# Output projection and last product with tokens on the partitions, and 8 of the last product's 22 K-tile pairs by seven block products for eight

## The chip, the cores and the metric

The kernel runs on one core of one Trainium2 chip. The core has a matrix engine (PE, whose loading of the stationary operand the profile lists apart as PEld), a vector engine (DVE), a scalar engine (ACT), a general engine (POOL) and an engine that issues DMAs (SP). They run side by side and wait for each other by semaphores. The metric is the device time of one execution in microseconds (us), smaller being better.

## The reference

One decoder layer for 256 tokens (S) of 2048 features (D), all float32. Only the last two of its products matter here:

```python
x = x + jnp.einsum('bsd,de->bse', merged, w_out[l])          # output projection, 2048 x 2048
h2 = rmsnorm(x, norm2_g[l])
u = causal_dwconv(jnp.einsum('bsd,df->bsf', h2, w_up[l]), conv_w[l], conv_b[l])
u_gate, u_val = u[..., :D_FF], u[..., D_FF:]                 # D_FF = 5632
x = x + jnp.einsum('bsf,fd->bsd', jax.nn.silu(u_gate) * u_val, w_down[l])   # last product, 5632 x 2048
```

Ahead of them stand a norm, the input projection, an attention, an mLSTM, gates and two projections, which the change leaves as they are.

## The kernel before

Every large product is made exact to float32 by three passes: each operand is split into a high part (its rounding to float32r) and a low part (the exact rest), and high times high, high times low and low times high are summed in PSUM. The activations' parts are made once. The weights' parts are made as the weights come: `load_chunk` fetches 1 MB (128 partitions x 2048 columns) into `raw`, of which there are three; `split_sub` makes two pieces of 1024 columns of it, ACT writing the high part `wh` (L104) and DVE the rest `wl` (L105), each of which also has three buffers; `next_sub` gives PE the next piece and has later ones loaded and split.

There are two forms of product. In the form of `block_a` the weights stand still in PE and the activations move: for a K-tile (128 rows of the sum) and 128 output columns, one matmul over 512 moving columns (high and low part of the 256 tokens side by side) and one over 256 (`wl` with the high part), in `products_a`; the result has output columns on the partitions, in two halves that are added. The branch gates (g), the branch projections (p), the output projection (wo), the first feed-forward product (up) and, written out by hand, the last product (y) have this form. In the form of `block_b` the activations stand still, 128 tokens at a time, and the weights move: for a K-tile, 128 tokens and 512 output columns, three matmuls over 512 columns each (`product_b`); the result has tokens on the partitions. The attention's fq, fk, fv and the mLSTM's mv have this form.

Stages of the end of the kernel. wo (L605 to L615): 16 blocks of 128 columns; DVE adds each to the residual `x2` (features on the partitions) and ACT and DVE make from it the operand `h2` of the next product, while POOL sums squares (`add_square`). up (L642 to L653): 88 blocks; DVE and ACT evacuate each (`up_evac`: sum of the halves, scale, three taps of the convolution), and from each pair of blocks one K-tile of the last product comes, in `g_tiles`. Two matmuls and a small product in PE make the norm's factor per token on every partition (`norm`, `as_rows`), between the first blocks. y (L656 to L675): four blocks of 512 output columns over 44 K-tiles; after each, DVE adds the result to `x2` and SP stores it.

Each engine works its instructions off in the order in which the program's scheduler left them, which is not quite the order of the code: it moves instructions ahead of others on which they don't depend. So a wait at the head of an engine's list holds what stands behind it.

Of the kernel before, what the change touches and what calls it, by code (L numbers as in the profile page):

```python
# [17 lines left out]
P = 128  # L18
# [23 lines left out]
def trunk(ctx: ExitStack, tc: tile.TileContext, a):  # L42
# [5 lines left out]
    work = ctx.enter_context(tc.tile_pool(name="work", bufs=2))  # L48
    psacc = ctx.enter_context(tc.tile_pool(name="psacc", bufs=4, space=bass.MemoryType.PSUM))
# [17 lines left out]
    # ---------------------------------------------------------------- weights, in order of use  # L67
    chunks = []

    def add_b(ap, n):  # L70
        for i in range(ap.shape[0]):
            chunks.append((ap[i], 4 * n))

    for i in range(8):
        chunks.append((a["w_mog0"][i], 2 * (MOG[0] + MOG[1])))
    add_b(a["w_mog1"], MOG[2])
    for name in ("w_fox", "w_mqk", "w_mv", "w_g", "w_p", "w_out", "w_up", "w_dn"):
        add_b(a[name], 512)

# [3 lines left out]
    def load_chunk(i, part=None):  # L83
        """Chunk i, whole or as its halves one by one."""
        if i >= n_chunk or (i in raws and part != 1):
            return
        src, n = chunks[i]
        if i not in raws:
            raws[i] = wpool.tile([P, 2048], F32, tag="raw", bufs=3, name=f"raw{i}")
        c = slice(0, n) if part is None else slice(part * n // 2, (part + 1) * n // 2)  # L90
        nc.sync.dma_start(raws[i][:, c], src[:, c])

    def split_sub(j):
        i, s = divmod(j, 2)
        if i >= n_chunk or j in subs:
            return
        load_chunk(i)
        if j < KD:
            put(hT[:, j, 0, :], hT[:, j, 1, :], xT[:, j, :], cst[:, C_G1 + j : C_G1 + j + 1])
        n = chunks[i][1] // 2  # L100
        raw = raws[i][:, s * n : (s + 1) * n]
        wh = wpool.tile([P, 1024], F32R, tag="wh", bufs=3, name=f"wh{j}")
        wl = wpool.tile([P, 1024], F32R, tag="wl", bufs=3, name=f"wl{j}")
        nc.scalar.activation(wh[:, :n], raw, AF.Copy)  # L104
        nc.vector.tensor_tensor(wl[:, :n], raw, wh[:, :n].bitcast(F32), ALU.subtract)  # L105
        subs[j] = (wh[:, :n], wl[:, :n])
# [3 lines left out]
    def next_sub():  # L110
        j = state["sub"]
        state["sub"] = j + 1
        for c in range(j // 2, j // 2 + 3):
            load_chunk(c)
        for q in range(j, j + 2):
# [20 lines left out]

    def mm(out, lhsT, rhs, start, stop):
        nc.tensor.matmul(out, lhsT, rhs, start=start, stop=stop)  # L138

    def product_b(outs, act, k, wh, wl, first, last):  # L140
        """outs[tok] += act[k].T @ w for both blocks of tokens; outs and w as lists over columns."""
        for tok in range(2):
            t = slice(tok * P, (tok + 1) * P)
            for o, w in zip(outs[tok], wh):
                mm(o, act[:, k, 1, t], w, first, False)
            for o, w in zip(outs[tok], wh):
                mm(o, act[:, k, 0, t], w, False, False)
            for o, w in zip(outs[tok], wl):
                mm(o, act[:, k, 0, t], w, False, last)
# [16 lines left out]
    def products_a(z, act, ks, wh, wl, first, last):  # L166
        """z += w.T @ act over the K-tiles ks: [columns, tokens], the low part's product apart."""
        for q, k in enumerate(ks):
            ws = slice(q * P, (q + 1) * P)
            mm(z, wh[:, ws], act[:, k].rearrange("p l s -> p (l s)"), first and q == 0, False)  # L170
            mm(z[:, :S], wl[:, ws], act[:, k, 0, :], False, last and q == len(ks) - 1)
# [16 lines left out]
    # ---------------------------------------------------------------- loads and constants  # L188
# [4 lines left out]
    hT = big.tile([P, KD, 2, S], F32R, tag="actT", bufs=2, name="hT")  # L193
# [5 lines left out]
    # The tensor engine's clock rises while it works: it works on zeros until the data is there.  # L199
# [27 lines left out]
    # A row of float32 values over tokens is added to a product by one bfloat16 pass: its three  # L227
    # bfloat16 parts are exact, head h's lying on partitions h, 32 + h and 64 + h.
# [11 lines left out]
    def bf16_parts(parts, rest):  # L240
        """Three bfloat16 parts that sum to rest exactly; rest is overwritten."""
# [5 lines left out]
    def rsqrt_mean(out, ss, n, tmp):  # L247
        """out = (ss / n + eps) ** -0.5"""
# [3 lines left out]
    # ---------------------------------------------------------------- norms over the features  # L252
# [4 lines left out]
    def add_square(x, first):  # L257
        """sq += x * x, the squares of a K-tile, to be summed over the partitions."""
# [7 lines left out]
    def norm(r):  # L266
        """r[token] = 1 / rms of the token's features."""
# [6 lines left out]
    def as_rows(r):  # L274
        """rb = the per-token values r on every partition."""
# [7 lines left out]
    # ---------------------------------------------------------------- input projection  # L283
# [3 lines left out]
    def gate_evac(z, n, at, c0):  # L287
        """The output gates of n columns, the first c0 of them being the heads' gates."""
# [23 lines left out]
    # Gates: log forget gates, their running sums F, and the mLSTM's running maximum.  # L312
# [6 lines left out]
    def gates_a():  # L319
# [8 lines left out]
        # log1p(e) = log(u) + (e - (u - 1)) / u  # L328
# [47 lines left out]
    att = big.tile([P, 8192], F32, tag="actT", bufs=2, name="att")  # L376
    qT = att[:, 0:2048].rearrange("p (h s) -> p h s", h=FH)
    kT = att[:, 2048:4096].rearrange("p (h s) -> p h s", h=FH)
    fv = att[:, 4096:6144].rearrange("p (t e) -> p t e", t=2)
    mqT = att[:, 6144:7168].rearrange("p (h s) -> p h s", h=MH)  # L380
    mkT = att[:, 7168:8192].rearrange("p (h s) -> p h s", h=MH)
# [46 lines left out]
    # ---------------------------------------------------------------- forgetting attention  # L428
# [53 lines left out]
    # ---------------------------------------------------------------- mLSTM inputs  # L482
# [91 lines left out]
    # ---------------------------------------------------------------- branch gates  # L574
# [9 lines left out]
    # ---------------------------------------------------------------- branch projections  # L584
    am = big.tile([P, 16, 2, S], F32R, tag="actT", bufs=2, name="am")
    for k in range(0, 16, 2):
        put(am[:, k : k + 2, 0, :], am[:, k : k + 2, 1, :], amT[:, k : k + 2, :])
# [4 lines left out]
    mT = big.tile([P, KD, 2, S], F32R, tag="actT", bufs=2, name="mT")  # L592
    for j in range(KD):
# [9 lines left out]
        put(mT[:, j, 0, :], mT[:, j, 1, :], ms[0])  # L603

    # ---------------------------------------------------------------- output projection  # L605
    x2 = big.tile([P, KD, S], F32, tag="r16", bufs=3, name="x2")
    for q in range(4):
        nc.gpsimd.dma_start(x2[:, 4 * q : 4 * q + 4, :], a["xT"][:, 4 * q : 4 * q + 4, :])
    h2 = big.tile([P, KD, 2, S], F32R, tag="actT", bufs=2, name="h2")
# [8 lines left out]
    g_tiles = []  # L618
    for n, tag, bufs in ((16, "actT", 2), (8, "r16", 3), (8, "r16", 3), (4, "og", 1), (4, "mv", 1)):
        t = big.tile([P, n, 2, S], F32R, tag=tag, bufs=bufs, name=f"ghl{len(g_tiles)}")  # L620
        g_tiles += [t[:, i] for i in range(n)]
    for i in range(4):
        g_tiles.append(work.tile([P, 2, S], F32R, tag="w2k", bufs=4, name=f"ghl{40 + i}"))
# [17 lines left out]

    ups = [block_a("up0", h2)]  # L642
    tasks.extend([lambda: norm(r2), lambda: as_rows(r2)])
    ups.append(block_a("up1", h2))
    for j in range(NF):
# [6 lines left out]
        nc.vector.tensor_tensor(t, sg, t, ALU.mult)  # L652
        put(g_tiles[j][:, 0, :], g_tiles[j][:, 1, :], t)  # L653

    # ---------------------------------------------------------------- feed-forward, second half
    for b in range(4):  # L656
        zs = [(acc_tile if b % 2 == 0 else aux_tile)(f"y{b}{i}") for i in range(4)]
        for c in range(NF // 4):
# [84 lines left out]
```

## Time and profile before

| | |
|---|---|
| median of three timed runs | 1412.65 us (1412.13 to 1412.81) |
| span of the profiled execution, the only time that its page gives of it | 1411.0 us |
| DVE, ACT, POOL busy | 935.6, 728.4, 64.5 us |
| output projection (wo), 512 matmuls | 581.48 to 672.11 us |
| first feed-forward product (up) | 672.11 to 1161.27 us |
| last product (y), 1408 matmuls | 1161.27 to 1406.63 us |
| weights loaded by SP's queue | 260.20 MB, 51.9% of the 16 DMA engines' time |

The stages' times are from the chain of work that ended last. In the list of groups a row gives line, engine, operation and tiles, the number of instructions, their busy time together, the mean of one in ns, and the idle time of the engine just before them with what ended it. In the timeline a row gives start and length in us. Matmuls overlap, so the mean of one is longer than the distance from one to the next; stages are counted by their starts.

### The profile page before, as it was taken

To read this page: it belongs to the slowest core of one execution; us is meant where nothing else is said; L and a number is where in the kernel's file an instruction comes from. 1 tells how busy PE (TensorE), PEld (TensorE's weight loads), DVE (VectorE), ACT (ScalarE), POOL (GpSimd) and SP (SyncE) were. 2 spreads that over 40 slices of the span, in tenths; PEclk is the share of its full clock that TensorE was granted. 3 is DMA by queue.
4 is the path that set the end of the run, shared out by engine and by line. 5 is a ranking of instruction groups with operands and counts; after the bars stand their busy time and mean duration, and the time that the engine had idled before them with its cause. 6 is when DMAs were issued, how large, how long until landed. Compare 5 with 4: busy or idle time off the path is not lost.

```text
span 1411.0 us, 20023 instructions
## 1 busy us (share of the span) xinstructions
PE 1401.3 (99%) x7847; PEld 1219.1 (86%) x7847; DVE 935.6 (66%) x1373; ACT 728.4 (52%) x1094; POOL 64.5 (5%) x92
## 2 busy tenths in 40 slices
PE   8999999999999999999999999999999999999998
PEld 7988888888888888888888888888888888888887
DVE  8556555557655577777778788877888884545453
ACT  7655544446544455555555555555555554333332
POOL 6001000000000011111000000000000000000000
PEclk9999999999999999999999999999999999999999
DMA  7645554444655554555455555555555555555562
GB/s 256 231 161 193 183 179 151 174 153 150 239 179 184 196 187 180 182 192 193 180 181 200 187 184 203 181 188 201 179 194 194 181 197 190 196 196 206 181 211 86
DMA packets 41230, 263.77 MB, mean 187 GB/s; under 512 B 4720, under 2 KB 6784, under 8 KB 10928
## 3 DMA queue, kind: packets, MB, share of 16 engines
q1 hardware_dynamic: 40320, 260.20, 51.9%
q0 software_dynamic: 672, 2.29, 0.5%
q8 instruction: 61, 1.00, 0.3%
q14 instruction: 33, 0.27, 0.1%
q10 hardware_dynamic: 144, 0.02, 0.0%
HBM read 260.39 MB, written 2.10 MB: 186 GB/s over the span
## 4 chain that ended last, share of the span: by engine, by line
PE 98%; DVE 1%; issue 0%; ACT 0%; DMA 0%; POOL 0%; DVEq 0%
PE up L138 35%; PE y L138 17%; PE g L138 12%; PE wo L138 6%; PE p L138 6%; PE fq L138 3%; PE mv L138 3%; PE fk L138 3%; PE fv L138 3%; PE mog L138 3%; PE mq L138 2%; PE mk L138 2%; PE ps_s L138 1%; PE ps_o L138 0%; PE ps_n L138 0%; DVE wl L105 0%
## 5 line engine op out<-in xcount | busy, mean ns | idle before, releaser
L105 DVE TENSOR_TENSOR wl<-raw,wh 128x1024 fp32r<-128x1024 f32 (+2 forms) x496 | 602.1, 1216 | 393.7 <-ACT wh L104 386.6
L104 ACT ACTIVATE wh<-raw 128x1024 fp32r<-128x1024 f32 (+2 forms) x496 | 519.2, 1047 | 639.5 <-PE y L138 142.8
L138 PE MATMUL up<-h,wh 128*128 128x512 f32 x1408 | 488.7, 391 | 0.0
L138 PE MATMUL up<-h,wl 128*128 128x256 f32 x1408 | 394.2, 280 | 0.0
L138 PEld LDWEIGHTS up<-h,wh 128*128 128x128 f32 x1408 | 263.3, 187 | 57.8
L138 PEld LDWEIGHTS up<-h,wl 128*128 128x128 f32 x1408 | 266.1, 189 | 0.0
L138 PE MATMUL y<-ghl,wh 128*128 128x512 f32 x704 | 221.1, 395 | 0.0
L138 PE MATMUL g<-hT,wh 128*128 128x512 f32 x512 | 182.6, 401 | 0.0
L138 PEld LDWEIGHTS y<-ghl,wl 128*128 128x128 f32 x704 | 132.3, 188 | 31.2
L138 PE MATMUL g<-hT,wl 128*128 128x256 f32 x512 | 143.8, 281 | 0.0
L138 PE MATMUL y<-ghl,wl 128*128 128x256 f32 x704 | 138.4, 278 | 0.0
L138 PEld LDWEIGHTS g<-hT,wh 128*128 128x128 f32 x512 | 96.2, 188 | 23.2
L138 PEld LDWEIGHTS y<-ghl,wh 128*128 128x128 f32 x704 | 107.1, 189 | 0.1
L138 PEld LDWEIGHTS g<-hT,wl 128*128 128x128 f32 x512 | 96.7, 189 | 0.1
L138 PE MATMUL wo<-mT,wh 128*128 128x512 f32 x256 | 90.6, 399 | 0.0
L138 PE MATMUL p<-am,wh 128*128 128x512 f32 x256 | 90.5, 399 | 0.0
L637 DVE SCALAR_TENSOR_TENSOR t<-u,cst,t 128x256 f32<-128x256 f32 x176 | 84.7, 481 | 4.5 <-ACT t L635 1.4
L138 PE MATMUL p<-am,wl 128*128 128x256 f32 x256 | 71.9, 281 | 0.0
L138 PE MATMUL wo<-mT,wl 128*128 128x256 f32 x256 | 71.7, 281 | 0.0
L138 PEld LDWEIGHTS wo<-mT,wh 128*128 128x128 f32 x256 | 48.1, 188 | 12.1 <-DVE mT L130 0.2
L138 PEld LDWEIGHTS p<-am,wh 128*128 128x128 f32 x256 | 48.1, 188 | 12.0
L635 ACT ACTIVATE t<-u,cst 128x256 f32<-128x256 f32 x88 | 51.7, 588 | 3.3 <-DVE u L632 1.9
(202 smaller groups left out, 1399.6 us busy)
## 6 DMA issues: line engine op xcount, KB each, us to landing
raw<-in_w_up SPq DMA_DIRECT2D x88, 1024.0 KB, 4.8
raw<-in_w_dn SPq DMA_DIRECT2D x44, 1024.0 KB, 4.8
raw<-in_w_g SPq DMA_DIRECT2D x32, 1024.0 KB, 4.8
raw<-in_w_fox SPq DMA_DIRECT2D x24, 1024.0 KB, 4.8
raw<-in_w_p SPq DMA_DIRECT2D x16, 1024.0 KB, 4.8
raw<-in_w_out SPq DMA_DIRECT2D x16, 1024.0 KB, 4.8
raw<-in_w_mqk SPq DMA_DIRECT2D x8, 1024.0 KB, 4.8
raw<-in_w_mv SPq DMA_DIRECT2D x8, 1024.0 KB, 4.8
```

The costliest lines, as they stand in the source:

```text
L104: nc.scalar.activation(wh[:, :n], raw, AF.Copy)
L105: nc.vector.tensor_tensor(wl[:, :n], raw, wh[:, :n].bitcast(F32), ALU.subtract)
L138: nc.tensor.matmul(out, lhsT, rhs, start=start, stop=stop)
L635: nc.scalar.activation(t, u[:, 2:], AF.Identity, scale=w[2], bias=w[3])
L637: nc.vector.scalar_tensor_tensor(out=t, in0=u[:, i : i + S], scalar=w[i], in1=t, op0=ALU.mult, op1=ALU.add)
```

## The change

wo and y are turned to tokens on the partitions. wo is four calls of `block_b`; the residual `x2` has tokens on the partitions, the squares are summed by ACT as it reads (`accum_out`), and what `h2` needs with features on the partitions comes from 32 transposes in PE (`transposed`). `x2` is also stored to a DRAM tile `xs` and read back in halves (`xr`) at the end, since its buffer is given to other data.

y has two halves of 1024 output columns. Its 44 K-tiles are taken in 22 pairs, as `Y_PAIRS` says: 14 ("p") in the plain way, 24 matmuls over 512 columns for each half; 8 ("S") as a product of 2 x 2 blocks (two K-tiles by two blocks of 128 tokens, times two K-tiles by two blocks of 512 columns) from seven block products for eight, so 21 matmuls for each half. For that, sums of the activations' blocks (`s2`, `s3`, `s4`, and a21 + a22 in place of a21) are made once in the up stage by DVE, split, and by way of the DRAM tile `s_dram` kept as `s_blocks`; and sums of the weights' blocks (`sums`) are made by DVE from each S chunk as it comes, so that an S chunk has four pieces: `b` (1024 columns as loaded), `b21` (512 as loaded), `t13` and `t24` (1024 each, of `sums`). Three PSUM tiles (products 5, 6, 7 and 1: `ps`) collect what several output blocks share, and are added to `xr` by nine instructions once for each half. The large operands are cut into eight tiles of four K-tiles each (`a8`) for two of sixteen.

```diff
+Y_PAIRS = "ppp" + "Sp" * 7 + "S" + "pppp"
...
+    for i in range(a["w_dn"].shape[0]):
+        kind = Y_PAIRS[i % len(Y_PAIRS)]
+        add_chunk(a["w_dn"][i], 2048, ("b", "b21", "t13", "t24") if kind == "S" else ("whole", "whole"))
...
+        if kind == "whole":
+            src = raw[:, s * n : (s + 1) * n]
+        elif kind == "b":
+            src = raw[:, 512:1536]
+            nc.vector.tensor_tensor(
+                sums[:, :1024].rearrange("p (i c) -> p i c", i=2),
+                raw[:, :512].unsqueeze(1).to_broadcast([P, 2, 512]),
+                src.rearrange("p (i c) -> p i c", i=2), ALU.subtract,
+            )
+        elif kind == "b21":
+            src = raw[:, 1536:]
+            nc.vector.tensor_tensor(sums[:, 1024:1536], raw[:, 1024:1536], sums[:, :512], ALU.subtract)
+        elif kind == "t13":
+            src = sums[:, :1024]
+            nc.vector.tensor_tensor(sums[:, 1536:], raw[:, 1536:], sums[:, 1024:1536], ALU.subtract)
+        else:
+            src = sums[:, 1024:]
...
-    for j in range(KD):
-        z = block_a(f"wo{j}", mT)
-        for h in (1, 0):
-            nc.vector.tensor_tensor(x2[:, j, :], x2[:, j, :], z[:, h * S : (h + 1) * S], ALU.add)
-        put(h2[:, j, 0, :], h2[:, j, 1, :], x2[:, j, :], cst[:, C_G2 + j : C_G2 + j + 1])
-        add_square(x2[:, j, :], j == 0)
...
+    def transposed(k):
+        ps = aux_tile(f"ps_h{k}")
+        for i in range(2):
+            for tok in range(2):
+                nc.tensor.transpose(
+                    ps[:, i * S + tok * P : i * S + (tok + 1) * P],
+                    x2[:, tok, (k + i) * P : (k + i + 1) * P], ident,
+                )
+        for i in range(2):
+            c = C_G2 + k + i
+            put(h2[k + i][:, 0, :], h2[k + i][:, 1, :], ps[:, i * S : (i + 1) * S], cst[:, c : c + 1])
+
+    for b in range(4):
+        z = block_b(f"wo{b}", mT, KD, 512)
+        cols = slice(b * 512, (b + 1) * 512)
+        for tok in range(2):
+            v = x2[:, tok, cols]
+            nc.vector.tensor_tensor(v, v, z[tok], ALU.add)
+            junk = work.tile([P, 512], BF16, tag="junk2", bufs=1, name="junk2")
+            nc.scalar.activation(junk, v, AF.Square, accum_out=ss2[:, tok, b : b + 1])
+        nc.gpsimd.dma_start(xs[:, :, cols], x2[:, :, cols])
+        tasks.extend([lambda k=4 * b: transposed(k), lambda k=4 * b + 2: transposed(k)])
...
+        if Y_PAIRS[m] == "S":
+            sv = scratch("sv", [P, 3 * P])
+            s2, s3, s4 = (sv[:, i * P : (i + 1) * P] for i in range(3))
+            nc.vector.tensor_tensor(s3, a21, a11, ALU.subtract)
+            nc.vector.tensor_tensor(a21, a21, a22, ALU.add)
+            nc.vector.tensor_tensor(s2, a21, a11, ALU.subtract)
+            nc.vector.tensor_tensor(s4, a12, s2, ALU.subtract)
+            se = big.tile([P, 2, 3 * P], F32R, tag="mv", name=f"se{m}")
+            put(se[:, 0], se[:, 1], sv)
+            nc.gpsimd.dma_start(
+                s_dram[:, n_s * 6 * P : (n_s + 1) * 6 * P], se.rearrange("p l c -> p (l c)")
+            )
+            n_s += 1
+        put(g_pairs[m][:, 0], g_pairs[m][:, 1], gv)
...
+            two([(ps[1], op(0, 0), first, last), (q[0][1], s4, False, False)])
+            two([(q[0][0], op(1, 0), False, False)])
+            two([(ps[5], op(0, 1), first, last), (ps[7], s3, first, last)])
+            two([(ps[6], s2, first, last), (q[1][0], op(1, 1), False, False)])
```

`two` takes the next piece of the weights and makes for each entry the three passes over 512 of its columns; a plain pair does the same for two K-tiles, two blocks of columns and two of tokens.

On DVE in the last product, before, one rest follows another, two for each chunk (`raw216`, `raw217` are chunks; the numbers of `wl` and `wh` are those of the pieces):

```order
L105 TENSOR_TENSOR wl433_11288<-raw216_11185,wh433_11287 128x1024
L105 TENSOR_TENSOR wl434_11308<-raw217_11243,wh434_11307 128x1024
L105 TENSOR_TENSOR wl435_11330<-raw217_11243,wh435_11329 128x1024
L105 TENSOR_TENSOR wl436_11350<-raw218_11285,wh436_11349 128x1024
L105 TENSOR_TENSOR wl437_11372<-raw218_11285,wh437_11371 128x1024
```

Now, from an S pair (its pieces t13 and t24 are 494 and 495) over a plain pair (496 and 497) to the next S pair (498 to 500 are its b, b21 and t13; its chunk is raw237):

```order
L139 TENSOR_TENSOR wl494_11895<-sums_10697,wh494_11894 128x1024
L123 TENSOR_TENSOR sums_10697<-raw237_11891 128x1024
L139 TENSOR_TENSOR wl495_11905<-sums_10697,wh495_11904 128x1024
L139 TENSOR_TENSOR wl496_11912<-raw236_11855,wh496_11911 128x1024
L139 TENSOR_TENSOR wl497_11922<-raw236_11855,wh497_11921 128x1024
L139 TENSOR_TENSOR wl498_11935<-raw237_11891,wh498_11934 128x1024
L130 TENSOR_TENSOR sums_10697<-raw237_11891,sums_10697 128x512
L139 TENSOR_TENSOR wl499_11952<-raw237_11891,wh499_11951 128x512
L133 TENSOR_TENSOR sums_10697<-raw237_11891,sums_10697 128x512
L139 TENSOR_TENSOR wl500_11971<-sums_10697,wh500_11970 128x1024
```

The first sum of the next S chunk (L123) stands ahead of the rest of this one's last piece (wl495); it writes the columns of `sums` that wl494 reads, and needs the chunk after the next, raw237.

On PE before, a K-tile of the last product has a pair of matmuls over 512 and a pair over 256 columns for each block of 128 output columns:

```order
L138 MATMUL y20_11717<-ghl36_6030,wh470_12079 128x512 x2
L138 MATMUL y20_11717<-ghl36_6030,wl470_12080 128x256 x2
L138 MATMUL y21_11718<-ghl36_6030,wh470_12079 128x512 x2
L138 MATMUL y21_11718<-ghl36_6030,wl470_12080 128x256 x2
L138 MATMUL y22_11719<-ghl36_6030,wh470_12079 128x512 x2
```

Now, at the end of the same S pair (p15, p16, p17 are the shared products 5, 6 and 7 of the second half, q the four output blocks), from the first use of t13:

```order
L178 MATMUL p15_11660<-wh494_11894,ghl8_5899 128x512 x2
L178 MATMUL p15_11660<-wl494_11895,ghl8_5899 128x512
L178 MATMUL p17_11661<-wh494_11894,s_ops1_10700 128x512 x2
L178 MATMUL p17_11661<-wl494_11895,s_ops1_10700 128x512
L178 MATMUL p16_11662<-wh495_11904,s_ops1_10700 128x512 x2
L178 MATMUL q110_11551<-wh495_11904,ghl8_5899 128x512 x2
L178 MATMUL q100_11549<-wh496_11911,ghl8_5899 128x512 x2
L178 MATMUL p16_11662<-wl495_11905,s_ops1_10700 128x512
L178 MATMUL q110_11551<-wl495_11905,ghl8_5899 128x512
```

Two matmuls of the plain pair that follows (wh496) have moved ahead of the two that need the rest of t24 (wl495).

On PE at the start of the up stage, now, the last transposes stand in the middle of the first block, and pieces of the second block (up1) between the uses of the operand tile that they fill, h23 (rows that only repeat are left out):

```order
L178 MATMUL up0_5910<-h21_5257,wl232_5873 128x256
L657 MATMUL ps_h12_5933<-ident_130,x2_5252 128x128 x4
L657 MATMUL ps_h14_5942<-ident_130,x2_5252 128x128 x4
L178 MATMUL up0_5910<-h22_5258,wh233_5913 128x512
L178 MATMUL up0_5910<-h22_5258,wl233_5914 128x256
L178 MATMUL up1_5971<-h20_5256,wh234_5951 128x512
L178 MATMUL up1_5971<-h20_5256,wl234_5952 128x256
L178 MATMUL up0_5910<-h23_5259,wh233_5913 128x512
L178 MATMUL up0_5910<-h23_5259,wl233_5914 128x256
```

Before, the first block went through its sixteen K-tiles without anything between them, and the small matmuls of `norm` followed in the second block.

More of the change, by code (lines that the diff above doesn't have):

```diff
@@ L135, in put, with operand @@
             )
+    def operand(name):
+        ts = [big.tile([P, 4, 2, S], F32R, tag="a8", bufs=8, name=f"{name}{i}") for i in range(4)]
+        return [ts[k // 4][:, k % 4] for k in range(KD)]
     def mm(out, lhsT, rhs, start, stop):
@@ L169, in products_a @@
             ws = slice(q * P, (q + 1) * P)
-            mm(z, wh[:, ws], act[:, k].rearrange("p l s -> p (l s)"), first and q == 0, False)
-            mm(z[:, :S], wl[:, ws], act[:, k, 0, :], False, last and q == len(ks) - 1)
+            mm(z, wh[:, ws], act[k].rearrange("p l s -> p (l s)"), first and q == 0, False)
+            mm(z[:, :S], wl[:, ws], act[k][:, 0, :], False, last and q == len(ks) - 1)
     def block_a(name, act, tasks_per_sub=1):
@@ L192, in trunk @@
     xT = big.tile([P, KD, S], F32, tag="r16", bufs=3, name="xT")
-    hT = big.tile([P, KD, 2, S], F32R, tag="actT", bufs=2, name="hT")
+    hT = operand("hT")
     for i in range(8):
@@ L582, in trunk @@
     run_tasks(len(tasks))
-    am = big.tile([P, 16, 2, S], F32R, tag="actT", bufs=2, name="am")
-    for k in range(0, 16, 2):
-        put(am[:, k : k + 2, 0, :], am[:, k : k + 2, 1, :], amT[:, k : k + 2, :])
+    am = operand("am")
+    for k in range(16):
+        put(am[k][:, 0, :], am[k][:, 1, :], amT[:, k, :])
     for g in range(2):
@@ L591, in trunk @@
             nc.scalar.activation(v, v, AF.Sigmoid)
-    mT = big.tile([P, KD, 2, S], F32R, tag="actT", bufs=2, name="mT")
+    mT = operand("mT")
     for j in range(KD):
@@ L618, in trunk @@
[L618 to L623, printed above, removed]
+        put(mT[j][:, 0, :], mT[j][:, 1, :], ms[0])
+    x2 = big.tile([P, 2, D], F32, tag="r16", bufs=3, name="x2")
+    xs = dram.tile([P, 2, D], F32, name="xs")
@@ new lines, in trunk @@
+    for b in range(4):
+        z = block_b(f"wo{b}", mT, KD, 512)
+        cols = slice(b * 512, (b + 1) * 512)
+        for tok in range(2):
+            v = x2[:, tok, cols]
[4 more added lines that the diff above has]
+        tasks.extend([lambda k=4 * b: transposed(k), lambda k=4 * b + 2: transposed(k)])
@@ L625, in trunk, with norm2 @@
+    def norm2():
+        ss, v = small("ss", [P, 2], 1), small("v", [P, 2], 1)
+        nc.vector.tensor_reduce(ss, ss2, AX.X, ALU.add)
+        rsqrt_mean(r2, ss, D, v)
+    g_pairs = []
+    for n, tag, bufs in ((2, "a8", 8),) * 4 + ((4, "r16", 3),) * 3 + ((2, "og", 1),):
+        t = big.tile([P, n, 2, 512], F32R, tag=tag, bufs=bufs, name=f"ghl{len(g_pairs)}")
+        g_pairs += [t[:, i] for i in range(n)]
+    s_dram = dram.tile([P, N_S * 6 * P], F32R, name="s_dram")
     ubuf = [const.tile([P, S + 2], F32, name=f"u{i}") for i in range(3)]
@@ L640, in up_evac @@
         return t
-    ups = [block_a("up0", h2)]
-    tasks.extend([lambda: norm(r2), lambda: as_rows(r2)])
+    ups = [block_a("up0", h2, 2)]
+    tasks.extend([norm2, lambda: as_rows(r2)])
     ups.append(block_a("up1", h2))
+    n_s = 0
     for j in range(NF):
@@ new lines, in trunk @@
+        nc.vector.tensor_tensor(gv[:, (j % 2) * S : (j % 2 + 1) * S], sg, t, ALU.mult)
+        if j % 2 == 0:
+            continue
+        m = j // 2
+        a11, a21, a12, a22 = (gv[:, i * P : (i + 1) * P] for i in range(4))
+        if Y_PAIRS[m] == "S":
[11 more added lines that the diff above has]
+            n_s += 1
@@ new lines, in trunk, with prod @@
+        put(g_pairs[m][:, 0], g_pairs[m][:, 1], gv)
+    sums = a8("sums", [2048])
+    s_blocks = []
+    for i in range(N_S * 6 // 16):
+        t = big.tile([P, 16 * P], F32R, tag="a8", bufs=8, name=f"s_ops{i}")
+        nc.gpsimd.dma_start(t, s_dram[:, i * 16 * P : (i + 1) * 16 * P])
+        s_blocks += [t[:, q * P : (q + 1) * P] for q in range(16)]
+    def prod(out, x, wh, wl, first, last):
+        hi, lo = x
+        mm(out, lo, wh, first, False)
+        mm(out, hi, wh, False, False)
+        mm(out, hi, wl, False, last)
@@ L737 @@
         ).ap()
-    aps["out"] = nc.dram_tensor("out_y", (D, S), F32, kind="ExternalOutput").ap()
+    aps["out"] = nc.dram_tensor("out_y", (S, D), F32, kind="ExternalOutput").ap()
     with tile.TileContext(nc) as tc:
```

158 lines of the change are left out of this document (105 added, 53 removed).

## The prediction

> **What bounds the kernel now.** The page comes first, its busy times and its chain of waits:
>
> ```profile
> PE 1401.3 (99%) x7847; PEld 1219.1 (86%) x7847; DVE 935.6 (66%) x1373; ACT 728.4 (52%) x1094; POOL 64.5 (5%) x92
> PE 98%; DVE 1%; issue 0%; ACT 0%; DMA 0%; POOL 0%; DVEq 0%
> ```
>
> PE works all the time and the chain that ends last is PE for 98% of it. A time saved or lost between two matmuls is a time saved or lost at the end; work on other engines counts only where PE comes to wait. So the stages' rates matter, and the chain in order of time has them (start, length, what, number of matmuls):
>
> ```profile
> 155.03 5.46 PE fv L138 x24
> 160.49 0.44 PE ps_k L388 x4
> 160.93 32.66 PE fv L138 x144
> ...
> 581.48 90.63 PE wo L138 x512
> ...
> 680.59 0.34 PE ps_norm L138 x4
> ...
> 1161.27 245.36 PE y L138 x1408
> 1406.63 0.02 issue
> 1406.65 0.75 DVE x L672 x2
> ```
>
> fv has the form to which wo and y are turned: 32.66 / 144 = 226.8 ns for a matmul over 512 columns. In y a pair over 512 and 256 columns, the same work as one and a half of those, takes 245.36 / 704 = 348.5 ns against 1.5 x 226.8 = 340.2; in wo 90.63 / 256 = 354.0 ns. What DVE has left beside PE is in the windows of up and y (core 0: length; busy of PE, PEld, DVE, ACT, POOL):
>
> ```profile
> 684.25:1161.27 477.02, 477.02 (x2753) 420.60 (x2753) 384.84 (x605) 277.34 (x434) 0.00 (x0) 1.00 0.53 190
> 1161.27:1406.63 245.36, 245.34 (x1408) 213.87 (x1407) 117.71 (x122) 92.66 (x90) 0.00 (x0) 1.00 0.52 183
> ```
>
> DVE is idle for 92 us of up and for over half of y; the granted clock is 1.00 in both.
>
> **The work of PE.** y afterwards: 14 plain pairs x 24 x 2 halves + 8 S pairs x 21 x 2 = 1008 matmuls over 512 columns. At 226.8 ns that is 228.6 us for 245.36: **-16.7 us**. Of this 48 x 0.2268 = 10.9 us is the eighth product left out, 5.8 us the form. wo: 4 blocks x 16 K-tiles x 6 = 384 x 0.2268 = 87.1 us, and eight groups of four transposes at 0.44 us (the row ps_k) are 3.5 us; together 90.6 for 90.63: **0.0**. The matmuls of `norm` go: **-0.3**.
>
> The page TensorE: Matmul & The Clock Gate of the Trainium skill, in Back-to-back issue gap, gives N / 2.4 + 2.5 ns for N moving columns (bfloat16). By it a pair would be 325 ns and one over 512 216 ns, so the form would bring nothing in wo and 0.7 us in y, and these three terms would come to about -8 us, an estimate. The rows disagree with it in both forms (348.5 and 226.8 ns), and the sum goes by the rows.
>
> **The feed of an S pair.** An S chunk has four pieces, and DVE makes three sums besides the rests. For a period of one S and one plain pair PE has 45 x 0.2268 = 10.21 us. DVE's load follows from these rows, the second group being three in succession:
>
> ```profile
> L130 DVE TENSOR_TENSOR am<-amT,am 128x512 fp32r<-128x512 f32 x8 | 5.4, 686 | 0.0
> L404 DVE TENSOR_TENSOR qn<-fq,qc 128x512 f32<-128x512 f32 x4 | 2.8, 692 | 0.1
> ...
> 492.04 1.23 DVE L105 TENSOR_TENSOR wl<-raw,wh 128x1024 fp32r<-128x1024 f32 x1 [1.60 <-ACT wh L104]
> 493.18 0.41 DVE L185 TENSOR_TENSOR sum<-sum,g 128x256 f32<-128x256 f32 x1
> 493.63 0.42 DVE L580 TENSOR_TENSOR gate<-sum,rb 128x256 f32<-128x256 f32 x1
> ```
>
> An instruction over 1024 columns takes 1.23 us, but the next starts after 1.14 if it needs nothing of it, and 0.04 us after its end if it does (493.63 after 493.59). Over 512 columns it is 0.69, some 0.60 to the next. Five rests and the sum L123 at 1.14 and three of 512 columns at 0.60 are 8.6 of 10.21 us: DVE isn't full. But the order decides. L123 of the next S chunk stands ahead of the rest of t24, and a piece can be split only when one of the three buffers is free. How fast that goes shows in fv, with the weights' matmuls of one piece, ACT's high part, the next piece, and DVE's rest:
>
> ```profile
> 179.15 0.62 PE L138 MATMUL fv<-wh,hT 128*128 128x512 f32 x2
> ...
> 179.80 1.06 ACT L104 ACTIVATE wh<-raw 128x1024 fp32r<-128x1024 f32 x1 [1.66 <-PE fv L138]
> 179.83 0.62 PE L138 MATMUL fv<-wh,hT 128*128 128x512 f32 x2
> 180.06 0.19 PEld L138 LDWEIGHTS fv<-wl,hT 128*128 128x128 f32 x1
> 180.28 0.39 PE L138 MATMUL fv<-wl,hT 128*128 128x512 f32 x1
> ...
> 180.89 1.23 DVE L105 TENSOR_TENSOR wl<-raw,wh 128x1024 fp32r<-128x1024 f32 x1 [1.49 <-ACT wh L104]
> ```
>
> The high part starts 0.03 us before PE begins the next piece, DVE 0.03 after ACT's end. With time 0 where PE begins piece b of an S pair: the high part of t13 runs from -0.03 to 1.03, its rest from 1.06 to 2.29, L123 (it overwrites what that rest reads) from 2.33, the rest of t24 1.14 behind it from 3.47 to 4.70. PE needs that rest after b (6 matmuls), b21 (3), t13 (6), four of t24 and the two moved ahead: 21 x 0.2268 = 4.76. From DVE's end to PE's next loading of weights it is 0.04 us, as these pieces of the chain have it, and a loading leads its matmul by 0.22 (180.06 and 180.28 above):
>
> ```profile
> 10.78 1.77 DVE wl L105
> 12.55 0.04 issue
> 12.59 1.28 PE mog L138 x7
> ```
>
> So the matmul due at 4.76 starts between 4.76 and 4.96. This is a knife's edge: 0 to 0.2 us in each of 14 periods; I take 0.12, **+1.7 us**. In the last S pair of each half an addition over 512 columns (0.69) stands there instead of L123, and nothing waits.
>
> How long L123 takes no row shows: float32, a block of 512 columns used twice as one operand. The nearest are wl (1.23, no repeated operand) and qn (0.69 for 512, with a repeated one, against 0.69 for am without). I take 1.23; twice that is the far end, and no row gives a reason for less. Every 0.1 us more is 14 x 0.1 = 1.4 us.
>
> **From wo to up.** The last two groups of transposes fill h23 in the middle of the first block, after its first 16 matmuls (8 x 0.354 = 2.83 us), and up0 needs it four K-tiles and three matmuls later: 2.83 + 0.87 + 1.42 + 0.57 = 5.7 us after wo's end. On DVE the factor per token stands ahead of it now:
>
> ```profile
> 681.21 0.72 POOL L250 TENSOR_TENSOR r<-v,mhalf 128x2 f32<-128x2 f32 x1 [6.22 <-DVE v L249]
> 681.96 0.48 DVE L278 TENSOR_SCALAR dg<-ident,r 128x128 f32<-128x128 f32 x2 [0.83 <-POOL r L250]
> 673.06 0.51 ACT L132 ACTIVATE h<-x,cst 128x256 fp32r<-128x256 f32 x1
> L637 DVE SCALAR_TENSOR_TENSOR t<-u,cst,t 128x256 f32<-128x256 f32 x176 | 84.7, 481 | 4.5 <-ACT t L635 1.4
> L129 ACT ACTIVATE am<-amT 128x512 fp32r<-128x512 f32 x8 | 4.7, 630 | 0.1
> L397 ACT ACTIVATION_READ_ACCUMULATOR junk<-fk,r 128x1 f32 x16 | 3.1, 194 | 0.0
> L249 DVE TENSOR_SCALAR qv<-qss 128x4 f32<-128x4 f32 x8 | 1.3, 163 | 0.0
> ```
>
> From wo's end: ACT's high part of piece 234 (to 1.0) and its two squares over 512 with their sums (0.82 each, to 2.7), DVE's two small instructions (3.1), POOL (3.9), `dg` (4.5), a rest over 1024 (5.7) and the first low part of h23 (6.2). PE waits some 0.5, and up to 0.2 to load: **+0.7**, within 0 (if DVE finds the factor early) and 1.5 (if two such waits follow each other).
>
> **What is hidden.** The operands' rests in up are
>
> ```profile
> L130 DVE TENSOR_TENSOR ghl<-t,ghl 128x256 fp32r<-128x256 f32 x44 | 18.4, 418 | 0.0
> ```
>
> and an S pair adds four DVE instructions over 128 columns (nearest, 256 columns: 0.41) and one over 384 (under 0.69): at most 2.3 us, 18.6 for all eight, and 22 rests over 512 for 44 over 256 give back 44 x 0.418 - 22 x 0.686 = 3.3. The 92 us of idle time cover it; a piece is split up to 2.8 us before PE needs it, so a burst of 2.3 passes. Uncovered it would cost up to 15 us. POOL loses `add_square`. The new DMAs (3 MB of `s_dram` stored and loaded, 2 MB of `xs` both ways) are 10 MB beside 260. At the end one DVE addition over 512 columns (0.69) takes the place of two (0.75), with a store of 256 KB for 128: **+0.2**, a choice between 0 and 0.5.
>
> **Sum.** -16.7 - 0.3 + 1.7 + 0.7 + 0.2 = -14.4, so a span of 1396.6 for 1411.0. The median of the runs shown is 1.65 us above that span; the same on top gives **1398.2 us**.
>
> **Rivals.** *Weights late, slower than before.* L123 needs a chunk whose load is issued only when the rest of the plain pair's second piece has freed its buffer, three rests behind the last L123. A period is thus at least 1.14 x 3 + 1.23 + 0.03 + landing = 4.68 + landing. How long loads take to land, in y, and while the residual came in by POOL's queue (here 2 MB at 369.74):
>
> ```profile
> DMA to landing us min/median/max: 4.7/4.8/6.7
> 369.74 2.18 POOL L608 DMA_DIRECT2D x<-in_xT  x4 [8.32 <-DVE am L130]
> DMA to landing us min/median/max: 8.4/8.4/8.4
> ```
>
> At 4.8 the bound is 9.5 us, under PE's 10.33 with the wait; it rules from 5.65, cancels the whole gain (14.4 / 14 = 1.03 a period) at 6.7, and at 8.4 costs 14 x 2.75 = 38 us: 1422 and more than before. Against it: the median; no POOL load runs in most periods, and the 3 MB of `s_ops` only at y's start. A chance of 0.09; with a landing of 6.9 us it gives 1398.2 + 14 x 1.25 = 1415.7.
>
> *L123 is slow.* At 1.6 us the wait is 0.49 a period: 1398.2 + 14 x 0.37 = 1403.4; at 2.26 the gain is gone. For it: a new operand form; against it: qn. 0.13.
>
> *The rate belongs to the stage, not the form.* y's matmuls keep 348.5 / 1.5 = 232.3 ns and wo's 236: y 234.2, wo 90.6 + 3.5; 1398.2 + 5.6 + 3.5 = 1407.3. For it: p and wo differ from y though their form is one. Against it: fv holds 226.8 over 144. 0.09. By the rule of the Trainium skill quoted above the forms don't differ, which speaks for this rival; the trace's two rates don't agree with it.
>
> *A single delay* (`s_ops` or the chunks beside it late at the first S pair, bursts in up): 2 to 6 us once, some 1402. 0.07.
>
> **How the numbers follow.** The forecast, 1395.5 to 1400.5, has 0.62. The range of 8 in 10 is **1395 to 1405**: the whole of the forecast, the single delay and most of the slow L123; it leaves out late weights and the stage's rate. Runs of this kernel tell 0.2% (2.8 us) from no change. Faster by more: 0.62 + 0.12 + 0.07 + 0.06 = **0.87**; within: 0.01 + 0.02 + 0.01 + 0.01 = **0.05**; slower: **0.08**.
>
> **What would show it.** Right: matmuls of q and p some 227 ns apart, 1008 of them in 229 to 232 us; PE waiting in y for `wl` about 14 times and no more than 0.2 us; wo in 90 to 91 us; L123 with a mean near 1230 ns; no wait of L123 for `raw`. Wrong: L123 waiting for DMAs, PE's waits in y above 0.3 us, a stall in up near an S pair, or a matmul above 230 ns.

## The result, and the profile after

The changed kernel takes **1395.41 us** (median of 4 runs, 1395.04 to 1395.92) for 1412.65; ratio 0.988, 95% interval 0.9866 to 0.9894. The profiled execution has a span of 1393.3 us. So by the spans 17.7 us are gained where 14.4 were forecast (17.2 by the medians). The time lies at the lower end of the range, 0.1 us below the forecast band of 1395.5 to 1400.5. First the page's busy times and its chain by engine:

```profile
PE 1384.7 (99%) x7347; PEld 1188.5 (85%) x7347; DVE 995.3 (71%) x1448; ACT 759.1 (54%) x1122; POOL 60.1 (4%) x92
PE 98%; DMA 1%; DVE 1%; ACT 0%; issue 0%; POOL 0%; DVEq 0%; ACTq 0%
```

PE is still the chain, with 500 matmuls less. What is new in it is 1% of DMA. Two windows, up and the last product (length; busy of PE, PEld, DVE, ACT, POOL; the counts take in one or two instructions that began before the window):

```profile
666.33:1155.97 489.64, 489.64 (x2827) 432.17 (x2826) 400.49 (x637) 288.58 (x432) 8.06 (x14) 1.00 0.57 200
1155.97:1388.71 232.74, 231.73 (x1010) 186.40 (x1008) 184.62 (x197) 118.84 (x124) 0.71 (x1) 1.00 0.57 207
```

The last product has its 1008 matmuls and takes 232.7 us for 245.5, though 230.3 were forecast; DVE's load in it rose from 117.7 to 184.6 us. Where the other gain comes from is in the chain of both kernels, in stages whose code is the same. Before:

```profile
366.65 124.37 PE g L138 x704
491.03 90.45 PE p L138 x512
```

After:

```profile
365.72 122.03 PE g L178 x704
487.76 88.75 PE p L178 x512
...
666.49 2.81 PE up L178 x16
669.30 0.87 PE ps_h L657 x8
670.17 8.51 PE up L178 x48
```

g and p give 2.3 and 1.7 us. A pair of matmuls (512 and 256 columns) took 124.37 / 352 = 353.3 ns and takes 122.03 / 352 = 346.7. These two rates are called rhythms below, the slow and the fast one; an interruption is any other work of PE, or a wait, between two pairs. Stage by stage, by the starts of first matmuls:

| | forecast | measured |
|---|---|---|
| all ahead of g (start at 297.99, now 297.02) | 0 | -1.0 |
| g, p | 0 | -2.3, -1.7 |
| wo | 0.0 | -0.6 |
| up, with `norm` and the handover | +0.4 | +0.5 |
| last product, work of PE | -16.7 | -16.9 (with e9's 228.65 us, which has no waits) |
| last product, waits | +1.7 | +4.1 |
| tail | +0.2 | +0.2 |
| sum | -14.4 | -17.7 |

Of the 1.0 us ahead of g, 0.7 are there at the first matmul of mq, an earlier product (192.76 for 193.43 us); a second profile of the changed kernel (e6) has 193.48 there, so they come and go between executions. The other 0.3 come in mq and mk, where some stretches have the fast rhythm now.

L123, the list of waits and the chain at the first S pair:

```profile
L123 DVE TENSOR_TENSOR sums<-raw 128x1024 f32<-128x1024 f32 x16 | 19.6, 1226 | 5.1 <-DMA raw<-in_w_dn 4.7
```

```profile
DVE sums L123 <- DMA raw<-in_w_dn: 4.7, 3, 3.8
PEld p L178 <- DVE wl L139: 4.3, 16, 0.8
```

```profile
1155.69 9.61 DMA raw<-in_w_dn
1165.29 0.02 issue
1165.32 0.07 DVE sums L123
...
1166.94 1.15 DVE wl L139
1168.09 0.04 issue
1168.13 5.38 PE q L178 x22
```

L123 takes 1.23 us, as taken. But it waited three times for its chunk, once for 3.8 us: the load that ended 0.03 us before it took 9.6 us to land, for 4.8 usually. The rest behind L123 on DVE came late for PE. Of a later period, the row of q and the next of its kind:

```profile
1199.47 5.25 PE q L178 x23
...
1209.79 2.31 PE q L178 x10
```

The period is 10.32 us for 10.20 of work.

### The profile page after: what moved, and what is told of

It is laid out like the page before. It is cut to its first block, busy times and chain, and to the rows that moved or that the text cites. A ratio compares the mean times of both kernels' runs of the same rounds, so it can differ in the third digit from the quotient of the medians.

```text
span 1393.3 us, 19175 instructions
## 1 busy us (share of the span) xinstructions
PE 1384.7 (99%) x7347; PEld 1188.5 (85%) x7347; DVE 995.3 (71%) x1448; ACT 759.1 (54%) x1122; POOL 60.1 (4%) x92
## 4 chain that ended last, share of the span: by engine, by line
PE 98%; DMA 1%; DVE 1%; ACT 0%; issue 0%; POOL 0%; DVEq 0%; ACTq 0%
PE up L178 35%; PE q L178 12%; PE g L178 12%; PE p L178 10%; PE wo L178 6%; PE mog L178 3%; PE fq L178 3%; PE mv L178 3%; PE fk L178 3%; PE fv L178 3%; PE mk L178 2%; PE mq L178 2%; DMA raw<-in_w_dn 1%; PE ps_s L178 1%; PE ps_o L178 0%; PE ps_n L178 0%
## 5 line engine op out<-in xcount | busy, mean ns | idle before, releaser
L138 ACT ACTIVATE wh<-raw 128x1024 fp32r<-128x1024 f32 (+2 forms) x496 | 512.2, 1033 | 539.2 <-PE up L178 120.6
L139 DVE TENSOR_TENSOR wl<-raw,wh 128x1024 fp32r<-128x1024 f32 (+2 forms) x496 | 590.1, 1197 | 296.2 <-ACT wh L138 291.3
L178 PE MATMUL q<-wh,ghl 128*128 128x512 f32 x512 | 156.3, 390 | 0.0
L178 PEld LDWEIGHTS q<-wh,ghl 128*128 128x128 f32 x512 | 96.1, 188 | 20.2
L178 PE MATMUL q<-wl,ghl 128*128 128x512 f32 x256 | 97.9, 391 | 0.6 <-DVE wl L139 0.6
L178 PE MATMUL wo<-wh,mT 128*128 128x512 f32 x256 | 79.5, 392 | 0.0
L178 PEld LDWEIGHTS q<-wl,ghl 128*128 128x128 f32 x256 | 47.4, 188 | 11.9 <-DVE wl L139 1.4
L139 DVE TENSOR_TENSOR wl<-sums,wh 128x1024 fp32r<-128x1024 f32 x32 | 39.1, 1223 | 24.7 <-ACT wh L138 24.7
L178 PEld LDWEIGHTS wo<-wh,mT 128*128 128x128 f32 x256 | 47.6, 188 | 9.6
L138 ACT ACTIVATE wh<-sums 128x1024 fp32r<-128x1024 f32 x32 | 33.9, 1061 | 38.2 <-PE q L178 38.2
```

The lines of the kernel that those rows point to most:

```text
L138: nc.scalar.activation(wh[:, :n], src, AF.Copy)
L139: nc.vector.tensor_tensor(wl[:, :n], src, wh[:, :n].bitcast(F32), ALU.subtract)
```

## Experiments

Two questions: why do g and p run faster, and what are the waits in the last product made of? "Distances" below are those between the starts of successive matmuls in the trace.

**e1, 32 bytes.** By the code, a new constant moves the tiles behind it up by 32 bytes. That shift alone, in the kernel before:

```diff
+    pad = const.tile([P, 8], F32, name="pad")
+    nc.gpsimd.memset(pad, 0.0)
```

> The kernel before, with 32 bytes more in the pool of constants, so that every tile behind it stands 32 bytes higher, as in the changed kernel; nothing else differs. In question: g, p and wo ran at 353.3 ns for a pair of matmuls (512 and 256 columns) before, and g and p at 346.7 ns in the changed kernel, whose code for them is the same. Theory A, the addresses decide: all three run at 346.7, so g 122.0 us (704 matmuls, for 124.4), p 88.75 (for 90.45), wo 88.75 (for 90.6), together 5.9 us less: 1406.8. Theory B, the phase with which PE's stream goes on after an interruption decides: no change that the addresses explain; each stage keeps whatever rhythm its last interruption left, most simply the old one, 1412.6 within 0.5.

1412.73 us (1412.1 to 1413.04, 10 runs), ratio 1.0001 (0.9992 to 1.0011); g, p and wo at 353.3 ns a pair. The 32 bytes are not it. Other changes of address aren't tested by this.

**e2, interruptions.** In the kernel before, ahead of blocks of p and within blocks of g, of eight kinds in turn:

```diff
+NUDGES = ((1, 1), (2, 1), (3, 1), (4, 1), (1, 128), (2, 128), (4, 128), (8, 1))
+        for _ in range(n):
+            mm(ps[:, :c], ones, ident[:, :c], True, True)
```

> The kernel before, with 1 to 8 small matmuls (1 or 128 columns, their result unused) put in the middle of each of the last 16 blocks of g and ahead of each of the 16 blocks of p, so that PE's stream of pairs is interrupted 32 times. Theory B (phase): after an interruption the pairs run at 353.3 or at 346.7 ns, both occur in the same stage at the same addresses, and each rhythm is kept without change until the next interruption; wo, which has none, keeps the rhythm of the last block of p. Theory A (addresses): every block of g and p keeps 353.3. The time itself is no measure: the small matmuls cost some 10 us.

Of the 32 stretches 12 ran at 346.7 and 20 at 353.3 ns, each without change to its end, in one program with its tiles at the same addresses. From the timeline of PE two stretches, with one other between them; of each its second pair and the pair twelve later:

```profile
478.62 0.39 PE L139 MATMUL g<-hT,wh 128*128 128x512 f32 x1
...
482.78 0.39 PE L139 MATMUL g<-hT,wh 128*128 128x512 f32 x1
...
491.06 0.39 PE L139 MATMUL g<-hT,wh 128*128 128x512 f32 x1
...
495.30 0.40 PE L139 MATMUL g<-hT,wh 128*128 128x512 f32 x1
```

4.16 / 12 = 346.7 ns, then 4.24 / 12 = 353.3. Six of the eight kinds were followed by either rhythm; the first and the seventh, (1, 1) and (4, 128), by the slow one all four times. In one point the expectation missed: wo didn't keep the rhythm of p's end, since it has a wait of its own (for `mT`, at 607).

**e3, all pairs plain.** The changed kernel with eight block products throughout:

```diff
-Y_PAIRS = "ppp" + "Sp" * 7 + "S" + "pppp"
+Y_PAIRS = "p" * 22
```

> The changed kernel with all 22 pairs of the last product plain, eight block products each; no sums, no s_dram. It shows what the form alone brings and what the eighth product left out brings. The prediction's terms: 48 x 2 x 11 = 1056 matmuls at 226.8 ns, 239.5 us for the last product, 5.8 us less than before, and no wait for the rests. Against the changed kernel's 232.7 us that is 6.8 us more: 10.9 us of products less 4.1 us of waits and their aftermath that go with the S pairs. Time: 1395.4 + 6.8 = 1402.2. Rival: if the S pairs' waits have another cause (the turned form, or the loads of the weights), they stay here, and the last product takes 243 us: 1406.

The last product is as expected:

```profile
1165.55:1405.08 239.53, 239.53 (x1058) 198.01 (x1056) 113.14 (x101) 92.79 (x90) 0.75 (x1) 1.00 0.53 191
```

The time has two values, on one chip: 1402.4 to 1402.7 in 3 runs, 1411.0 to 1412.2 in 7 (0.9971 of before over all, 0.9951 to 0.9991). In the profiled execution, one of 1411.3 us, up ran at 353.3 ns a pair. Its 1408 pairs at 6.6 ns more are 9.3 us. Without them the time is 1402.0, for 1402.2 expected; that up was fast in the 3 quicker runs is read from their times.

**e4, the order on DVE.** The two halves of `sums` take turns:

```diff
+            odd = Y_PAIRS[: (i - n_chunk) % len(Y_PAIRS)].count("S") % 2
+            r0, r1 = (sums[:, 1024 * h : 1024 * h + 1024] for h in (odd, 1 - odd))
...
-                sums[:, :1024].rearrange("p (i c) -> p i c", i=2),
+                r0.rearrange("p (i c) -> p i c", i=2),
```

> The changed kernel with the two halves of the tile of sums in turn: an S chunk's first sum (L123) goes into the half that the last piece (t24) of the S chunk before reads, so it can't stand ahead of that piece's rest; it stands behind the rests of the plain pair. The same instructions otherwise. Theory (the order on DVE): PE's 14 waits of 66 to 73 ns for the rest of t24 go, and the slow ten matmuls behind each (some 55 ns): 1.7 us; as the chunk is needed 3 us later, the waits of L123 for raw at 1165 and 1217 cost less, up to 2.2 us more with their aftermath. 1395.4 - 1.7 = 1393.7, down to 1391.3. Rival: DVE's load, not its order, makes PE wait: then the waits move to another piece and the time stays at 1395.4 within 0.6.

1394.35 us once and 1403.64 to 1403.71 three times: up again has both rhythms, here the slow one in the chain (483.26 / 1367.5 = 353.4), and the window of the last product:

```profile
679.82 483.26 PE up L181 x2735
```

```profile
1165.84:1397.37 231.53, 230.40 (x1010) 186.87 (x1008) 184.49 (x197) 118.69 (x124) 0.71 (x1) 1.00 0.57 208
```

The 14 waits are gone, but 196 of its 1007 distances still lie between 229 and 242 ns (213 in the changed kernel), and the late chunk now costs one wait of 1.3 us. Many of the longer distances stand behind loadings of weights that still waited for a rest on DVE (16 of p, 2.8 us together), mostly without holding up their matmul. So 1.2 us were gained in the last product for 1.7 at least expected.

**e5, a chosen interruption.** Six matmuls over 256 columns, as written, in the kernel before, in g:

```diff
+        for _ in range(6):
+            mm(ps[:, :S], ones, cst[:, :S], True, True)
```

> The kernel before, with one interruption more: six float32 matmuls over 256 columns (result unused, 1.3 us) in the first block of the second half of g. The interruptions of this kind, the six of ps_n and the two of ps_rb, were followed by the rhythm of 346.7 ns a pair in every case of the kernel before. Theory B (the last interruption sets the rhythm, and it is kept): from there g, p and wo run at 346.7 instead of 353.3, g 352 x 2 pairs less 8, p 256, wo 256 pairs, together 5.5 to 5.9 us less for 1.3 more: 1408.2. What the changed kernel gained in g and p is so to be had without the change. Rival (the rhythm has its cause in what runs on the other engines or in the addresses): no gain, 1413.9.

The expectation failed: 1415.37 us (1413.7 to 1422.8, 10 runs; ratio 1.0032, 1.0016 to 1.0049). After the interruption g went on at 87.62 / 248 = 353.3:

```profile
403.51 2.59 PE ps_settle L138 x12
406.10 87.62 PE g L138 x496
```

A float32 matmul as written is two on PE, so the six are twelve. They took 2.59 us for the 1.3 expected, and that is the whole loss (1415.37 - 1412.82 of the kernel before beside it = 2.55). They were also not quite of the kind intended, since an interruption by ps_n is six on PE and 1.30 us long. Three runs near 1422.7 and one at 1413.7 have no profile, and stay unexplained.

**e6, the changed kernel again.**

> The changed kernel once more, unchanged. E3 and e4, which share its code up to the last product, ran up in either of the two rhythms from one execution to the next (499.1 or 489.8 us). If that is a matter of chance in each execution, runs of 1404.7 us turn up here beside those of 1395.4. Rival: something in e3 and e4 decides it (their constants stand elsewhere, the code has another length), and here all runs lie at 1395.4 within 0.6, as the four did.

1395.72 to 1396.63 in 4 runs (ratio 0.9883, 0.9867 to 0.99), in the middle 0.9 us above the first four. Up was at 346.7 in both profiles, and by their times in all eight executions. So not every program has shown both rhythms: e3, e4 and e9 have, each on one chip, this one hasn't, and the kernel before kept to one time (1411.9 to 1413.2) in its 52 runs beside these experiments.

**e7, rests asked for later.** e4, with the passes of a piece in another order, and e5's matmuls (twelve on PE) in up's third block:

```diff
-                    prod(o, x, wh[:, c], wl[:, c], f, l)
+                    mm(o, lo, wh[:, c], f, False)
+                    mm(o, hi, wh[:, c], False, False)
+                for i, (o, (hi, lo), f, l) in enumerate(todo):
+                    mm(o, hi, wl[:, i * 512 : (i + 1) * 512], False, l)
```

> e4 with two changes. First, in each piece of an S pair the passes with wh of both products stand ahead of the passes with wl, so PE asks for a piece's rest after four matmuls instead of two (0.45 us later). Theory: the weights' loads of PE that wait some 0.1 us for the rest of t13 or t24 no longer wait, and with them go the ten or so matmuls at 232 instead of 227 ns behind each: the last product falls from 231.5 to about 230.1 us, what is left being the one wait for the late chunk at 1177 (1.3 us). Rival: the slow matmuls belong to the S pairs (their operands, s_ops, or their accumulators), then it stays at 231.5. Second, six float32 matmuls over 256 columns (1.3 us) in the third block of up; by theory B up then runs at 346.7 ns a pair in every execution: 1394.35 - 1.4 + 1.3 = 1394.3 in all runs, none near 1403.6. Rival: chance stays, and both times turn up.

The last product takes 230.45 us, and 21 of 1006 distances are above 228 ns, as expected. The added matmuls did the reverse of what was expected: up had begun at 346.7 and went on at 353.3 (480.42 / 1359.5), by the times in all four runs (1404.75 to 1405.45):

```profile
682.91 2.59 PE ps_settle L181 x12
685.50 480.42 PE up L181 x2719
```

**e8, a third of `s_ops` later.** The third load at the start is left out, and instead:

```diff
+            if b == 0 and m in (6, 7, 8, 9):
+                c = (m - 6) * 512
+                raw = raws[n_chunk - 2 * len(Y_PAIRS) + m]
+                nc.gpsimd.tensor_copy(t[:, c : c + 1], raw[:, :1])
+                nc.gpsimd.dma_start(t[:, c : c + 512], s_dram[:, 32 * P + c : 32 * P + c + 512])
```

> e7 with the last third of s_ops (1 MB of 3) loaded in four parts beside the seventh to tenth pair of the last product instead of at its start. Theory: raw207 took 9.6 and 10.1 us to land because it shared the DMA engines with the 3 MB of s_ops; with 2 MB it lands some 2 us earlier, and the first sum, which waits for it, and the rest behind it on DVE are in time: the wait of 1.3 us goes, 1393.0. Rival: the parts loaded later delay chunks there, and a wait of the same size moves to the seventh to tenth pair: 1394.3.

1403.57 us (1403.26 to 1403.72), with the slow rhythm of e7; the last product takes 228.70 us, 1.75 less than e7's. The chunk of the first sum landed in 8.5 us for 10.4, the sum's wait for it fell from 4.6 to 2.6 us, and PE has none left.

**e9, e8 without the added matmuls in up.**

> e8 without the six matmuls in up, which there were followed by the slow rhythm (353.3 ns a pair for the rest of up) against what was expected of them. The last product stays at 228.7 us. Up: if the interruption by ps_rb is followed by 346.7 ns, as in all eight executions of the changed kernel, 489.8 us and 1396.1 (e6, same day) - 233.1 + 228.7 = 1391.7 in all; if by 353.3, 499.1 us and 1401.0. Which it is, is not foretold by the theory (the rhythm is set by the phase, in a way not known): both are allowed, other times are not.

1391.96 us once, 1400.85 to 1401.49 three times: both values as foretold. Last product 228.65 us. Two of its periods:

```profile
1187.47 5.67 PE q L181 x25
...
1197.67 5.67 PE q L181 x25
```

10.20 us, 45 x 226.7 ns: no wait, and one distance of 1007 above 228 ns.

**e10, e11, widths grouped.** In e9, and in the kernel before (there in wo and the last product too), a piece's matmuls over 512 columns first:

```diff
             mm(z, wh[:, ws], act[k].rearrange("p l s -> p (l s)"), first and q == 0, False)
+        for q, k in enumerate(ks):
+            ws = slice(q * P, (q + 1) * P)
             mm(z[:, :S], wl[:, ws], act[k][:, 0, :], False, last and q == len(ks) - 1)
```

> e9 with another order in the pairs of mq, mk, g, p and up: the eight matmuls over 512 columns of a piece first, then its eight over 256, instead of in turn. Theory C: a matmul takes 226.7 ns over 512 and 113.4 over 256 columns, 340.2 a pair, and what the pairs take above that (6.6 or 13.2 in turn, 8.2 in groups of two as in the last product before, 16.4 for each round of four) is the price of changes between the two widths; with one round in sixteen matmuls it is 16.4 / 8 = 2 ns a pair: 342.3, and no two rhythms. 1408 + 512 + 256 + 128 pairs save 4.4 ns each against the fast rhythm: 10 us, 1391.7 - 10.1 = 1381.6. Up takes 482 to 484 us. Rival: the price belongs to each matmul over 256 columns (the next weights take about 190 ns to load, longer than it runs): then eight in succession take longer, up to 190 ns each, and up takes 1408 x (226.7 + 190) = 587 us, the kernel 1490; if only the pitch seen in the last product before holds (115), 481.6 us.

> The kernel before with the same order: the eight matmuls over 512 columns of a piece, then its eight over 256, in mq, mk, g, p, wo, up, and in the last product. By theory C every pair takes 342.3 ns: the last product 704 x 0.3423 = 241.0 us for 245.4; up 483 for 489.3; g, p and wo 11 ns a pair less, 5.6, 2.8 and 2.8 us (less in the first third of g, which is interrupted): together 21 us, 1391.5. Then what the turned form brought by its rate in the last product (5.8 us) was four fifths a matter of the changes of width. Rival: as for e10; up 587, y 293 us.

Theory C falls: 1398.62 us (1398.3 to 1399.62) for 1381.6 expected, and 1414.08 (1413.32 to 1414.67, 10 runs; ratio 1.0008, 0.9999 to 1.0018) for 1391.5. From the timeline of e10:

```profile
800.50 1.11 PE L181 MATMUL up<-h,wl 128*128 128x256 f32 x8
801.45 2.00 PE L181 MATMUL up<-h,wh 128*128 128x512 f32 x8
803.29 1.12 PE L181 MATMUL up<-h,wl 128*128 128x256 f32 x8
```

A piece takes 803.29 - 800.50 = 2.79 us, 349 ns a pair, neither rhythm of before, and up 493.8 us. The eight over 256 columns take 0.95 us to the next start, 113 ns at first, then 119 and 120; the eight over 512 take 1.84, the first five of them 228 to 236 ns, the others 226 to 227. Against 113.4 and 226.7 each, a piece is 72 ns longer: 45 in the matmuls over 256, and only 27 in those over 512 that follow a change of width. So the change of width isn't the main price; the rival's 190 ns is wrong too. In e10 PE again waits 1.4 us for the rest behind the late first chunk, so e8's cure of that wait has little margin.

**e12, twos in up.** e9, with up in the order of the last product before:

```diff
+        n = 2 if act is h2 else 1
+        for q0 in range(0, len(ks), n):
+            for q in range(q0, q0 + n):
```

> E9 with the matmuls of up in groups of two, as those of the last product of the kernel before: two over 512 columns, then two over 256. That form took 348.4 ns a pair in every profile of the kernel before and its variants (y 245.5 us in each), and showed no second rhythm. Theory: with it up takes 1408 x 348.4 = 490.6 us and a little for its start, in every execution; g and p are left as they are and stay at 346.7. The kernel takes 1391.96 (e9 in its fast rhythm, up at 346.7) + 1408 x 1.7 ns = 1394.4 in all runs, with no run near 1401. Rival: groups of two have two rhythms too, and only luck has shown one: then some runs lie 9 us away.

1394.13 us, 1393.82 to 1394.55 in all four runs (ratio 0.9871, 0.9855 to 0.9888). Up runs at 479.32 / 1376 = 348.3 ns a pair:

```profile
679.62 479.32 PE up L182 x2752
```

It costs 2.2 us against e9's one run in the fast rhythm, and four runs have shown one time only. They are below the changed kernel's eight (1395.0 to 1396.6) too, but the intervals of the two ratios overlap, so a difference isn't shown.

## Why the prediction came out as it did

*The mechanism of the gain held.* The work of PE in the last product was right term by term: the form 6.0 us (245.5 to e3's 239.5) for 5.8, the product left out 10.9 (e3's 239.5 to e9's 228.65) for 10.9. The rate goes with the form, so the rival "stage, not form" falls. The formula that the prediction quoted beside it, from Back-to-back issue gap on the page TensorE: Matmul & The Clock Gate of the Trainium skill, is given there for a single matmul by itself; the streams here (226.7 and 348.5 ns) don't follow it.

*The knife's edge held in its place; its size was partly luck.* 0.12 us were taken for each of 14 periods; the period is 10.32 us for e9's 10.20. Its make-up was not foreseen: some 66 ns are the wait, the rest are some ten matmuls at 232 ns, behind it and behind the loading for the rest of t13. In the last S pair of each half, where nothing was to wait, PE waited 0.09 us too. That the order of the work and not DVE's load is the cause, e4 and e7 show together with the same DVE work: the first takes away the waits, the second the slow matmuls.

*L123* took 1226 ns for the 1230 taken; the rival "L123 is slow" falls.

*Weights late, and the single delay.* "L123 waiting for DMAs" was named as a sign of error, and it came, but in 3 of 16 cases, all in the first half; so did a second sign, waits of PE above 0.3 us. The first is the chunk that landed in 9.6 us while the 3 MB of `s_ops` came in. The second, 0.2 us, is its echo: that chunk was issued late, at 1170.9 us, and landed in the usual 4.8. The third is the rival's bound at work, once: the chunk issued at 1211.5 us took 6.2 us to land, 4.68 + 6.2 = 10.9 against a period of 10.3, and PE waited 0.55 us. Why it took 6.2 is open; POOL's queue moved nothing then.

```profile
raw<-in_w_dn SPq DMA_DIRECT2D x1, 1024.0 KB, 6.2
```

So the two rivals were right in their mechanism, and smaller than priced. In the sum they stood with nothing: the waits and their aftermath came to 4.1 us (232.74 - 228.65) for 1.7. Of these 4.1, e4's order took away 1.2, e7's later demand 1.1, and the moved third of `s_ops` 1.8.

*wo and the handover* were mis-sized. Six of the eight groups of transposes fall into wo, two into up (0.87 us). So the +0.5 of up for +0.4 agrees by luck: it holds these 0.87, which the sum had in wo, while the loading that waits for h23 waits 0.2 us in place of the 0.7 taken.

*The step that failed* stands in no term: the sum takes for granted that the stages whose code isn't touched keep their time. g and p brought 4.0 us, since from their last interruption, at 366 us, on they ran in the faster of two rhythms; that is no part of the forecast mechanism. Without these 4.0 the gain would have been 13.7 us, 0.7 less than forecast, so the range would have held, but the agreement of the whole hides errors of either sign. The reach of the rhythm is larger: up, with 1408 pairs, has the same two 9.3 us apart, and close relatives of the changed kernel (e3, e4, e9) fell into the slow one in most runs. The prediction had no case for that.

What stays open: what in an interruption decides the rhythm, and so why the change put g and p into the fast one. A shift by 32 bytes (e1), the kind of interruption alone (e2) and its having been followed by one rhythm before (e5, e7) don't foretell it.

## What to carry to other kernels

Before a gain of some us is put down to an edit, compare the stages that it doesn't touch, by their time for one repetition; a rate that changes there is a cause of its own, and one profile may show only one of its values. An instruction that waits for a transfer belongs behind the work that doesn't; and a consumer that asks for the late half of a pair last gains the slack at no cost (e7). Where a stream of matmuls has two rhythms, a slightly slower order that has shown only one (e12, four runs) can be worth more than the faster rhythm of a lucky profile.

## What the hardware showed unexpectedly

Pairs over 512 and 256 columns ran at 346.7 or 353.3 ns, at a granted clock of 1.0, and kept the value over up to 1376 pairs, until an interruption. In the slow rhythm the two distances of a pair repeat over three pairs, 232 + 118, 240 + 120 and 236 + 114 ns (g before); in up the fast one is 230 + 117 from pair to pair. Nothing here explains either. The page TensorE: Matmul & The Clock Gate of the Trainium skill, in LDWEIGHTS, gives a loading time of columns / 1.2, 107 ns for 128, which would hide behind a matmul over 256 columns (113 ns). The rows for bfloat16 operands come near it (98 to 100 ns, identb and sel), the others don't: a loading for the large products lasts 187 to 190 ns, one for the transposes 138 to 140, and the closest distance that matmuls over 256 columns kept up in e10 is 120.

A loading of PE that waits for a semaphore costs more than its wait: the ten or so matmuls behind it stood mostly 231 to 236 ns apart instead of 227, also where the wait was too short to hold up the matmul itself (e4). Without such waits (e3, e9) one distance in a thousand was longer than 228. Distances of 228 to 236 also stand behind each group of matmuls over 256 columns in e10, where nothing waits.
